# A two-layer decoder trunk with top-k experts: the experts' gate and spill loads asked for by ScalarE's queue, products and dots queued behind named work, one group fewer done ahead, index copies on VectorE

## The chip, the cores and the metric

The kernel runs on one core of one Trainium2 chip. The metric is the device time of one execution in microseconds (us). In the profile PE is TensorE, with its weight loads apart as PEld, DVE is VectorE, ACT is ScalarE, POOL is GpSimd and SP is SyncE, which in this kernel only asks for DMA transfers (rows of a queue itself are marked SPq, ACTq and so on).

## The reference

The input is one sequence of 512 tokens with 1024 channels. Two layers each have a mixer (pooling beside retention in layer 0, a gated linear recurrence in layer 1) and a PEER block; a layer norm closes each. The change lies in the PEER block:

```python
def block(xt):                                             # 128 tokens
    q = (xt @ w_q).reshape(T, PEER_HEADS, 2, PEER_HALF)    # 8 heads, 2 halves of 128
    s = jnp.einsum('thpd,hpkd->thpk', q, sub_keys)         # scores against 128 sub-keys
    s_top, i_top = lax.top_k(s, PEER_TOPK)                 # 16 best of each half
    cand = ...                                             # 16 x 16 sums, and their expert numbers
    best, pos = lax.top_k(cand, PEER_TOPK)                 # 16 best of 256
    eid = jnp.take_along_axis(cand_id, pos, axis=-1)       # one of 128*128 experts
    gate = jax.nn.softmax(best, axis=-1)
    act = gelu(jnp.einsum('td,thkd->thk', xt, u_tab[eid]))
    coef = gate * act
    return jnp.einsum('thk,thkd->td', coef, v_tab[eid])
```

Each token so takes part in 8 x 16 = 128 of the 16,384 experts. An expert is one row of `peer_u` (its dot with the token, then Gelu) and one row of `peer_v` (added to the output with the coefficient).

## The kernel before

Tokens stand in four blocks `tb` of 128. The experts of the first 384 tokens are computed densely: the 16,384 experts are 128 blocks of 128, four blocks make a group `g` (`NB` = 4, 32 groups). For every block, `mm1` multiplies 128 rows of `peer_u` with the tokens on TensorE (24 matmuls of 128x352, since each product is three products of high and low parts), and ScalarE's Gelu puts the activations into `ge`. `mm2` (L1084) later multiplies coefficients with 128 rows of `peer_v`: 18 matmuls of 128x512 a block, into six accumulators of PSUM that stay open over all 128 blocks. Rows of the two tables stream in through `stream`: SP asks for a block of 512 KB (`raw`, five buffers), ScalarE rounds it to `hi` (L168) and VectorE forms the rest `lo` (L169).

The last 128 tokens (`tb` = 3) are not dense: `gather_rounds` takes one expert of each token per round. GpSimd gathers 128 rows of `peer_u` (L967), VectorE takes the dots into a column of `av` (L978); after eight rounds ScalarE's Gelu and one multiply make the coefficients `cf` (L981, L982); GpSimd gathers the rows of `peer_v`, and VectorE accumulates them (L988) eight rounds after their dots. The first 32 tokens' activations come from a third path, `Scatter`: in the top-k stage, VectorE takes dots of gathered rows `urow` (L104), and GpSimd adds the gates into a table `gz` in memory.

A PEER block has these stages. `route_topk` (L766) goes through four chunks `c` of heads: projection of the queries (the copies `qh` of PSUM at L780 are ScalarE's), scores of four token blocks, top 16 by VectorE (L859 to L863), the copy of the indices to 16-bit floats `itop` (L864, ScalarE), and for `tb` = 1, 2, 3 some of the chunk's eight `Scatter` dots, which are to follow the last top-k instruction. `route_gates` (L882) then builds the dense gates of the other tokens with one-hot matmuls (L909, L910), scales them into `gbuf` (L911) and writes them to the table `gd` in memory (L915). Beside both, `lookahead` (L755) does `mm1` for the first `NLA` = 20 groups; it is advanced by one block for every 2.8 units of cost that the two stages hand out. Its `ge` are written to `sp` in memory (L763), but for the last two groups, which are kept.

`experts` (L991) then goes through all groups in an order that mixes the old ones with the 12 fresh ones, whose `mm1` is done here. `fetch` gets a group's data two groups ahead: `ge` from `sp` (L1022), gates from `gd` (L1024) and from `gz` (L137) into `gt`. For each pair of blocks VectorE multiplies `gt` by `ge` (L1050, the pair product), ScalarE rounds the result to `ch` (L168) and VectorE forms the rest `cl` (L169); with `hi` and `lo` these are what `mm2` reads. `gt` has three buffers, `ch` and `cl` two each. After each block, gather rounds are let in so that they end with the blocks.

The order of the instructions on each engine is set by a scheduler from the traced program. `with tc.issue_after(x)` forces each instruction that is traced inside, on the engine of `x`, to stand behind `x` in that engine's queue. An engine works through its queue in order, so an instruction that waits holds all behind it, DMA requests included.

Of the kernel before, what the change touches and what calls it, by code (L numbers as in the profile page):

```python
# [9 lines left out]
F32 = mybir.dt.float32  # L10
# [4 lines left out]
AF = mybir.ActivationFunctionType  # L15
ALU = mybir.AluOpType
# [4 lines left out]
P = 128  # L21
# [14 lines left out]
QN = P // NU  # L36
QC = 32 // QN
GQ = 8
NSD = TD // 32
NLA = 20  # L40
NSZ = 4
KEEP = 2
ROT = 3
# [98 lines left out]
class Kern:  # L142
# [623 lines left out]
    def route_topk(self, layer, xT, kT, gz):  # L766
        nc, tc, io = self.nc, self.tc, self.io
        with tc.tile_pool(name="rt", bufs=1) as rt, tc.tile_pool(name="rt2", bufs=2) as rt2, \
# [6 lines left out]
            itop = rt.tile([P, NTB, 16, 16], F16, name="itop", tag="itop")  # L775
# [65 lines left out]
            for c in range(4):  # L841
                qs = []
                keys = rt2.tile([P, 4, P], F32, name="keys", tag="keys")
                nc.sync.dma_start(out=keys, in_=io["keysT"][layer][:, c * 4:c * 4 + 4, :])
                self.proj_T(wq, c, xT, sink_q, early=c == 0)
                for tb in range(NTB):
                    ts = slice(tb * P, (tb + 1) * P)
                    ps = self.psB.tile([P, 512], F32, name="pB", tag="pB")
                    for i in range(4):
                        nc.tensor.matmul(ps[:, i * P:(i + 1) * P], qs[i][:, ts], keys[:, i, :],  # L850
                                         start=True, stop=True)
                    ixs = rs2.tile([P, 4, 16], U32, name="ix", tag="ix", bufs=2)
                    for i in range(4):
                        hp = c * 4 + i
                        sc = ps[:, i * P:(i + 1) * P]
                        mx = stop[:, tb, hp, :]
                        ix = ixs[:, i, :]
                        s2 = rs2.tile([P, P], F32, name="s2", tag="s2")
                        nc.vector.max(out=mx[:, 0:8], in_=sc)  # L859
                        nc.vector.max_index(out=ix[:, 0:8], in_max=mx[:, 0:8], in_values=sc)  # L860
                        nc.vector.match_replace(out=s2, in_to_replace=mx[:, 0:8], in_values=sc, imm_value=NEG)
                        nc.vector.max(out=mx[:, 8:16], in_=s2)
                        top = nc.vector.max_index(out=ix[:, 8:16], in_max=mx[:, 8:16], in_values=s2)  # L863
                    nc.scalar.copy(itop[:, tb, c * 4:c * 4 + 4, :], ixs)  # L864
                    yield YC[c]
                    if tb == 0:
                        yield from choose(0, c * 2, 2)
                        if c:
                            gz.add(self)
                    else:  # L870
                        n = (2, 3, 3)[tb - 1] * QC // 8
                        yield 1.3 * n
                        with tc.issue_after(top.ins):
                            gz.dots(self, n)
                gz.weigh(self, rs2)
                if c == 0:
                    gz.add(self)
# [80 lines left out]
    def gather_rounds(self, layer, main, ga):  # L958
        nc, io = self.nc, self.io
        eid, gate, x, acc = main  # L960
        jobs = list(range(P))
        coefs = []

        def row(name, job):
            t = ga.tile([P, D], F32, name="row", tag="row", bufs=6)
            at = eid[:, job:job + 1]
            nc.gpsimd.indirect_dma_start(out=t, out_offset=None, in_=io[name],  # L967
                                         in_offset=bass.IndirectOffsetOnAxis(ap=at, axis=0))
            return t

        for n in range(len(jobs) + GQ):
            if n < len(jobs):
                j = jobs[n]
                k = n % GQ
                if k == 0:
                    av = ga.tile([P, GQ], F32, name="av", tag="av", bufs=2)
                ur = row("u%d" % layer, jobs[n])
                nc.vector.tensor_tensor_reduce(ur, ur, x, 1.0, 0.0, ALU.mult, ALU.add, av[:, k:k + 1])  # L978
                if k == GQ - 1:
                    cf = ga.tile([P, GQ], F32, name="cf", tag="cf", bufs=2)  # L980
                    nc.scalar.activation(cf, av, AF.Gelu)  # L981
                    nc.vector.tensor_tensor(cf, cf, gate[:, j - k:j + 1], ALU.mult)  # L982
                    coefs.append(cf)
            if n >= GQ:
                i = n - GQ
                vr = row("v%d" % layer, jobs[i])
                c = coefs[i // GQ][:, i % GQ:i % GQ + 1]
                nc.vector.scalar_tensor_tensor(acc, vr, c, acc, ALU.mult, ALU.add)  # L988
            yield

    def experts(self, layer, xT, hs, gd, gz, sp, norm):  # L991
        nc, tc, io = self.nc, self.tc, self.io
        with tc.tile_pool(name="ex", bufs=2) as ex, tc.tile_pool(name="ga", bufs=2) as ga:
            ex.tile([P, 48], F32, name="gap", tag="gap")
            accs = [[(self.psC if hf else self.psB).tile([P, 512], F32, name="pC" if hf else "pB",
                                                          tag="pC" if hf else "pB") for hf in range(2)]
                    for _ in range(3)]
            rounds = self.gather_rounds(layer, (self.eid, self.gate3, self.x3, hs[3]), ga)
            total = NLA * NB * 1.0 + (NE - NLA * NB) * 2.0
# [13 lines left out]
            def fetch(n):  # L1013
                if n >= NG:
                    return
                g = order[n]
                if g in kept:
                    ge = self.kept[g]
                else:
                    ge = self.pe.tile([P, NB, TN], F32, name="ge", tag="ge", bufs=3)  # L1020
                if g < NLA and g not in kept:
                    nc.sync.dma_start(out=ge, in_=sp[g])  # L1022
                gt = ex.tile([P, NSD, NB, 32], F32, name="gt", tag="gt", bufs=3)
                nc.sync.dma_start(out=gt[:, NSZ:], in_=gd[g])  # L1024
                gz.read(nc.gpsimd if n < 2 else nc.sync, gt[:, :NSZ], g)
                ges[g] = (ge, gt)

            def front(i):
# [13 lines left out]
            for i in range(NE):  # L1042
# [4 lines left out]
                if i % 2 == 0:  # L1047
                    ge, gt = ges[g]
                    gf = gt[:, US:, b:b + 2, :]
                    nc.vector.tensor_tensor(gf, gf, ge[:, b:b + 2, :].rearrange("p b (s t) -> p s b t", t=32), ALU.mult)  # L1050
                    ch = ex.tile([P, 2, TD], F32R, name="ch", tag="ch")
                    cl = ex.tile([P, 2, TD], F32R, name="cl", tag="cl")
                    s4 = "p b (s t) -> p b s t"
                    cf = gt[:, :, b:b + 2, :].rearrange("p s b t -> p b s t")
                    mark = self.split(cf, ch.rearrange(s4, t=32), cl.rearrange(s4, t=32))
                    cs += [(ch[:, 0], cl[:, 0]), (ch[:, 1], cl[:, 1])]
                v = self.stream(io["peer_v"][layer, g * NB + b])
                vs.append(v)
# [2 lines left out]
                        for tb in range(3):  # L1061
                            self.mm2(accs[tb], tb, cs[k], vs[k], k == 0, False)
                used += 1.0 if g < NLA else 2.0
                while done < (P + GQ) * used / (total * 1.02):
                    done += 1
                    with tc.issue_after(mark.ins):
                        next(rounds, None)
            for _ in rounds:
                pass
            for tb in range(3):  # L1070
# [146 lines left out]
```

## Time and profile before

| | |
|---|---|
| Runs | 2842.74, 2844.35, 2854.67 us, median 2844.35 us |
| Profiled execution | 2857.61 us, its span 2855.8 us |
| Busy share of the span | PE 97%, PEld 86%, DVE 82%, POOL 47%, ACT 39% |
| Stages of layer 0 (us from the span's start) | mixer to 181, top-k 181 to 445, gates 445 to 622, change-over 622 to 649, experts 649 to 1367 |
| The same stages of layer 1 | to 1650, to 1920, to 2098, to 2126, to 2842 |

The ends of the stages are taken from the first and last matmuls of each stage; the change-over lies between the last gate matmul and the first `mm2`. TensorE is busy nearly throughout, so the idle time that counts is what stands ahead of its instructions. The other engines' busy shares say little by themselves: they matter where a matmul waits for them.

### The profile page before, as it was taken

To read this page: it belongs to the slowest core of one execution; us is meant where nothing else is said; L and a number is where in the kernel's file an instruction comes from. 1 tells how busy PE (TensorE), PEld (TensorE's weight loads), DVE (VectorE), ACT (ScalarE), POOL (GpSimd) and SP (SyncE) were. 2 spreads that over 40 slices of the span, in tenths; PEclk is the share of its full clock that TensorE was granted. 3 is DMA by queue.
4 is the path that set the end of the run, shared out by engine and by line. 5 is a ranking of instruction groups with operands and counts; after the bars stand their busy time and mean duration, and the time that the engine had idled before them with its cause. 6 is when DMAs were issued, how large, how long until landed. Compare 5 with 4: busy or idle time off the path is not lost.

```text
span 2855.8 us, 41883 instructions
## 1 busy us (share of the span) xinstructions
PE 2766.2 (97%) x15314; PEld 2451.5 (86%) x15314; DVE 2352.5 (82%) x4524; ACT 1111.9 (39%) x1607; POOL 1328.6 (47%) x865
## 2 busy tenths in 40 slices
PE   9999999999999999999999999998999999999998
PEld 7898899998888898788788888998998888787886
DVE  6777889868888787888797777898878887888888
ACT  3353346553333333333334343445543333333332
POOL 0005567764555544554000016667754554555552
PEclk9999999999999999999999999999999999999999
DMA  6457776999999998999222556676999999999995
GB/s 224 136 172 215 207 226 187 250 282 359 377 382 371 362 381 342 345 384 352 96 82 71 211 169 192 195 235 173 275 317 362 371 392 352 353 377 361 383 371 191
DMA packets 318895, 791.24 MB, mean 277 GB/s; under 512 B 62176, under 2 KB 128224, under 8 KB 318688
## 3 DMA queue, kind: packets, MB, share of 16 engines
q1 hardware_dynamic: 198560, 485.34, 47.4%
q0 software_dynamic: 120128, 303.22, 31.3%
q8 instruction: 120, 1.97, 0.3%
q14 instruction: 87, 0.71, 0.1%
HBM read 709.94 MB, written 78.51 MB: 276 GB/s over the span
## 4 chain that ended last, share of the span: by engine, by line
PE 47%; issue 22%; DVE 12%; DMA 12%; POOL 6%; ACT 1%; SPq 0%; DVEq 0%; POOLq 0%; ACTq 0%
PE pA L184 8%; PE pA L186 8%; PE pA L185 8%; POOL row L967 6%; DMA row<-in_v,eid 5%; PE pB L1084 5%; PE pC L1084 5%; DVE lo L169 3%; PE pC L184 3%; PE pC L185 3%; PE pC L186 3%; DMA gt<-gz 2%; DMA ge<-sp 2%; DVE row L978 1%; DVE h L988 1%
## 5 line engine op out<-in xcount | busy, mean ns | idle before, releaser
L168 ACT CAST hi<-raw 128x1024 fp32r<-128x1024 f32 (+1 forms) x609 | 634.4, 1049 | 767.1 <-DMA raw<-in_peer_v 303.5
L169 DVE TENSOR_TENSOR lo<-raw,hi 128x1024 fp32r<-128x1024 f32 (+1 forms) x609 | 731.4, 1216 | 135.2 <-ACT hi L168 111.5
L967 POOL DMA_INDIRECT row<-in_u,eid x256 | 390.4, 1525 | 548.9 <-DVE av L978 504.7
L186 PE MATMUL pA<-xThi,lo 128*128 128x352 f32 (+2 forms) x1840 | 620.2, 337 | 16.3 <-DVE lo L169 16.3
L184 PE MATMUL pA<-xThi,hi 128*128 128x352 f32 (+2 forms) x1840 | 624.4, 339 | 10.6 <-ACT qh L780 7.6
L185 PE MATMUL pA<-xTlo,hi 128*128 128x352 f32 (+2 forms) x1840 | 620.1, 337 | 0.7 <-DVE xTlo L169 0.7
L126 POOL DMA_INDIRECT gz<-gate,idx x256 | 484.6, 1893 | 137.9 <-issue 73.2
L967 POOL DMA_INDIRECT row<-in_v,eid x256 | 368.4, 1439 | 109.4 <-issue 59.1
L186 PEld LDWEIGHTS pA<-xThi,lo 128*128 128x128 f32 x1840 | 349.4, 190 | 35.1 <-DVE lo L169 20.2
L184 PEld LDWEIGHTS pA<-xThi,hi 128*128 128x128 f32 x1840 | 350.0, 190 | 30.5 <-ACT qh L780 8.5
L185 PEld LDWEIGHTS pA<-xTlo,hi 128*128 128x128 f32 x1840 | 349.8, 190 | 17.5 <-DVE xTlo L169 1.2
L988 DVE SCALAR_TENSOR_TENSOR h<-row,cf,h 128x1024 f32<-128x1024 f32 x256 | 329.1, 1286 | 35.9 <-DMA row<-in_v,eid 35.5
L1084 PE MATMUL pB<-hi,cl 128*128 128x512 f32 x768 | 303.9, 396 | 31.5 <-DVE cl L169 31.5
L978 DVE CUSTOM_DVE_ANT_0 row<-row,x 128x1024 f32<-128x1024 f32 x256 | 311.2, 1219 | 6.0 <-DMA row<-in_u,eid 5.8
L1084 PE MATMUL pB<-lo,ch 128*128 128x512 f32 x768 | 300.3, 391 | 3.9 <-DVE lo L169 3.9
L1084 PE MATMUL pB<-hi,ch 128*128 128x512 f32 x768 | 300.3, 391 | 1.4 <-ACT ch L168 1.4
L1084 PE MATMUL pC<-hi,cl 128*128 128x512 f32 x768 | 300.1, 391 | 0.0
L1084 PE MATMUL pC<-hi,ch 128*128 128x512 f32 x768 | 300.1, 391 | 0.0
L1084 PE MATMUL pC<-lo,ch 128*128 128x512 f32 x768 | 300.0, 391 | 0.0
L1050 DVE TENSOR_TENSOR gt<-gt,ge 128x704 f32<-128x704 f32 x128 | 111.4, 888 | 176.7 <-DMA gt<-gz 88.2
L168 ACT CAST ch<-gt 128x768 fp32r<-128x768 f32 x128 | 107.0, 836 | 272.4 <-DVE gt L1050 192.2
L740 POOL DMA_INDIRECT urow<-in_u,ids x64 | 74.9, 1170 | 292.0 <-ACT ids L86 196.5
(280 smaller groups left out, 4603.8 us busy)
## 6 DMA issues: line engine op xcount, KB each, us to landing
raw<-in_peer_ut SPq DMA_DIRECT2D x256, 512.0 KB, 6.4
raw<-in_peer_v SPq DMA_DIRECT2D x256, 512.0 KB, 7.6
gd<-gbuf SPq DMA_DIRECT2D x16, 2048.0 KB, 10.6
gt<-gd SPq DMA_DIRECT2D x64, 512.0 KB, 9.3
sp<-ge SPq DMA_DIRECT2D x36, 704.0 KB, 4.8
ge<-sp SPq DMA_DIRECT2D x36, 704.0 KB, 11.5
raw<-in_peer_w_q SPq DMA_DIRECT2D x32, 512.0 KB, 5.5
gz<-zero SPq DMA_DIRECT2D x64, 256.0 KB, 4.5
```

What stands on the lines that cost most here:

```text
L126: d = nc.gpsimd.indirect_dma_start(out=flat, out_offset=bass.IndirectOffsetOnAxis(ap=self.idx[c][:, j:j + 1], axis=0), in_=gate[:, j:j + 1 ...
L168: self.nc.scalar.copy(hi, src)
L169: return self.nc.vector.tensor_tensor(lo, src, hi.bitcast(F32), ALU.subtract)
L184: nc.tensor.matmul(ps, ah, bh, start=(first and i == 0), stop=False)
L185: nc.tensor.matmul(ps, ah, bl, start=False, stop=False)
L186: nc.tensor.matmul(ps, al, bh, start=False, stop=(last and i == n - 1))
L740: d = self.nc.gpsimd.indirect_dma_start(out=t, out_offset=None, in_=self.io["u%d" % layer], in_offset=bass.IndirectOffsetOnAxis(ap=ids[:, ...
L967: nc.gpsimd.indirect_dma_start(out=t, out_offset=None, in_=io[name], in_offset=bass.IndirectOffsetOnAxis(ap=at, axis=0))
L978: nc.vector.tensor_tensor_reduce(ur, ur, x, 1.0, 0.0, ALU.mult, ALU.add, av[:, k:k + 1])
L988: nc.vector.scalar_tensor_tensor(acc, vr, c, acc, ALU.mult, ALU.add)
L1050: nc.vector.tensor_tensor(gf, gf, ge[:, b:b + 2, :].rearrange("p b (s t) -> p s b t", t=32), ALU.mult)
L1084: nc.tensor.matmul(acc[hf], a[:, ts], b[:, hf * 512:(hf + 1) * 512], start=first and i == 0, stop=last and i == 2)
```

## The change

It has six parts.

1. `NLA` goes from 20 to 19: four blocks of `mm1` per layer move from `lookahead` into `experts`, and one group fewer is written to `sp` and read back.
2. The copy of the top-k indices to `itop` goes from ScalarE to VectorE (32 instructions).
3. The eight `Scatter` dots of a chunk are let in as 0, 4, 4 after the top-k of `tb` = 1, 2, 3, instead of 2, 3, 3.
4. In `gather_rounds`, Gelu and `cf` of eight dots are traced two rounds after the last dot, not at once, and the accumulation comes `LAG` = 12 rounds after its dot, not 8.
5. From the third group on, `fetch` asks for `ge`, `gd` and `gz` through ScalarE's queue, not SP's: 154 requests in the program.
6. The pair product stands in VectorE's queue behind the first gather dot after the previous pair's `cl`, or behind that `cl` where no dot follows.

```diff
-NLA = 20
+LAG = GQ + 4
+NLA = 19
...
-                    nc.scalar.copy(itop[:, tb, c * 4:c * 4 + 4, :], ixs)
+                    nc.vector.tensor_copy(itop[:, tb, c * 4:c * 4 + 4, :], ixs)
...
-                        n = (2, 3, 3)[tb - 1] * QC // 8
+                        n = (0, 1, 1)[tb - 1] * QC // 2
                         yield 1.3 * n
                         with tc.issue_after(top.ins):
                             gz.dots(self, n)
...
-        for n in range(len(jobs) + GQ):
+        for n in range(len(jobs) + LAG):
+            dot = None
...
-                nc.vector.tensor_tensor_reduce(ur, ur, x, 1.0, 0.0, ALU.mult, ALU.add, av[:, k:k + 1])
+                dot = nc.vector.tensor_tensor_reduce(ur, ur, x, 1.0, 0.0, ALU.mult, ALU.add, av[:, k:k + 1])
                 if k == GQ - 1:
-                    cf = ga.tile([P, GQ], F32, name="cf", tag="cf", bufs=2)
-                    nc.scalar.activation(cf, av, AF.Gelu)
-                    nc.vector.tensor_tensor(cf, cf, gate[:, j - k:j + 1], ALU.mult)
-                    coefs.append(cf)
-            if n >= GQ:
-                i = n - GQ
+                    dots.append((av, j - k))
+            if dots and n - dots[0][1] == GQ + 1:
+                a, j = dots.pop(0)
+                cf = ga.tile([P, GQ], F32, name="cf", tag="cf", bufs=2)
+                nc.scalar.activation(cf, a, AF.Gelu)
+                nc.vector.tensor_tensor(cf, cf, gate[:, j:j + GQ], ALU.mult)
+                coefs.append(cf)
+            if n >= LAG:
+                i = n - LAG
...
-            yield
+            yield dot
...
+                q = nc.scalar if n > 1 else nc.sync
                 if g < NLA and g not in kept:
-                    nc.sync.dma_start(out=ge, in_=sp[g])
+                    q.dma_start(out=ge, in_=sp[g])
                 gt = ex.tile([P, NSD, NB, 32], F32, name="gt", tag="gt", bufs=3)
-                nc.sync.dma_start(out=gt[:, NSZ:], in_=gd[g])
-                gz.read(nc.gpsimd if n < 2 else nc.sync, gt[:, :NSZ], g)
+                q.dma_start(out=gt[:, NSZ:], in_=gd[g])
+                gz.read(q if n > 1 else nc.gpsimd, gt[:, :NSZ], g)
...
-                    nc.vector.tensor_tensor(gf, gf, ge[:, b:b + 2, :].rearrange("p b (s t) -> p s b t", t=32), ALU.mult)
+                    with ExitStack() as after:
+                        if i:
+                            after.enter_context(tc.issue_after(turn.ins))
+                        nc.vector.tensor_tensor(gf, gf, ge[:, b:b + 2, :].rearrange("p b (s t) -> p s b t", t=32),
+                                                ALU.mult)
...
-                    mark = self.split(cf, ch.rearrange(s4, t=32), cl.rearrange(s4, t=32))
+                    turn = mark = self.split(cf, ch.rearrange(s4, t=32), cl.rearrange(s4, t=32))
...
-                while done < (P + GQ) * used / (total * 1.02):
+                while done < (P + LAG) * used / (total * 1.02):
                     done += 1
                     with tc.issue_after(mark.ins):
-                        next(rounds, None)
+                        dot = next(rounds, None)
+                    if turn is mark and dot is not None:
+                        turn = dot
```

Lines after the first edits stand a little lower in the changed kernel: L1050 becomes L1059, L1084 becomes L1096, L1022 and L1024 become L1028 and L1030, L168 and L169 become L169 and L170.

Three places show how the queues change. The first is VectorE early in the experts stage of layer 0. Before, three products stand close together, one on `gt_7157` and two on the next group's `gt_7544` (the numbers tell the buffers of different groups apart), and only behind them the `cl` that reads `gt_7157`:

```order
L169 TENSOR_TENSOR lo_7485<-raw_7482,hi_7484 128x1024
L988 SCALAR_TENSOR_TENSOR h3_87<-row_7539,cf_7216,h3_87 128x1024
L169 TENSOR_TENSOR lo_7497<-raw_7494,hi_7496 128x1024
L1050 TENSOR_TENSOR gt_7157<-gt_7157,ge_7156 128x11x64
L1050 TENSOR_TENSOR gt_7544<-gt_7544,ge_7542 128x11x64 x2
L169 TENSOR_TENSOR lo_7555<-raw_7552,hi_7554 128x1024
L169 TENSOR_TENSOR cl_7549<-gt_7157,ch_7548 128x768
```

Now a product is followed by its own `cl`, and a gather dot (L980) stands between a `cl` and the next product:

```order
L170 TENSOR_TENSOR lo_7719<-raw_7716,hi_7718 128x1024
L1059 TENSOR_TENSOR gt_7402<-gt_7402,ge_7400 128x11x64
L170 TENSOR_TENSOR lo_7756<-raw_7753,hi_7755 128x1024
L170 TENSOR_TENSOR lo_7768<-raw_7765,hi_7767 128x1024
L170 TENSOR_TENSOR cl_7750<-gt_7402,ch_7749 128x768
L980 ISA row_7759,av_7487<-row_7759,x3_1031 128x1024
L980 ISA av_7487 128x1
L993 SCALAR_TENSOR_TENSOR h3_87<-row_7762,cf_7539,h3_87 128x1024
L170 TENSOR_TENSOR lo_7810<-raw_7807,hi_7809 128x1024
L1059 TENSOR_TENSOR gt_7402<-gt_7402,ge_7400 128x11x64
L170 TENSOR_TENSOR cl_7873<-gt_7402,ch_7872 128x768
```

No product of a later group stands ahead of the `cl` any more, and the two products on `gt_7402` have the first one's `cl` and a dot between them.

The second place is the queue that asks for the gates, in the same stage. Before, SP's queue has them between the table's blocks:

```order
L174 DMA raw_8521<-in_peer_ut 128x1024
L1024 DMA gt_8363<-gd0_1024 128x1024
L137 DMA gt_8363<-gz0_1420 128x512
L174 DMA raw_8558<-in_peer_v 128x1024
L174 DMA raw_8570<-in_peer_v 128x1024
```

Now they stand in ScalarE's queue between the roundings:

```order
L169 CAST ch_7477<-gt_7027 128x768
L169 CAST hi_7574<-raw_7572 128x1024
L1030 DMA gt_7552<-gd0_1024 128x1024
L138 DMA gt_7552<-gz0_1420 128x512
L169 CAST hi_7621<-raw_7619 128x1024
L169 CAST hi_7633<-raw_7631 128x1024
L169 CAST ch_7556<-gt_7151 128x768
```

The request for `gt_7552` now follows the `ch` of the group whose buffer it takes (`gt_7027`), with one rounding between them.

The third place is TensorE where layer 0 goes over from the gates to `mm2`. Before, a whole block of `mm1` begins behind the last gate matmul (L910):

```order
L909 MATMUL pC<-og,oh 128x128
L910 LDWEIGHTS oh
L910 MATMUL pC<-og,oh 128x128
L184 MATMUL pC<-xThi,hi 128x352
L185 MATMUL pC<-xTlo,hi 128x352
```

Seven blocks follow there, 168 matmuls, and then the first `mm2`. Now:

```order
L910 MATMUL pC<-og,oh 128x128
L911 LDWEIGHTS oh
L911 MATMUL pC<-og,oh 128x128
L187 MATMUL pA<-xThi,lo 128x352
L185 MATMUL pA<-xThi,hi 128x352
L186 MATMUL pA<-xTlo,hi 128x352
```

Here the last matmul of a block and three blocks follow, 73 matmuls, ahead of the first `mm2`: the blocks taken from `lookahead` are missing at this place, and the gates stage ahead of it has 1847 matmuls of `mm1` where it had 1848 (counted from the start of top-k).

More of the change, by code (lines that the diff above doesn't have):

```diff
@@ L961, in gather_rounds @@
         jobs = list(range(P))
-        coefs = []
+        coefs, dots = [], []
         def row(name, job):
```

## The prediction, made before the changed kernel was run

> **What bounds the kernel now.** I read the page's first lines, then the stages one by one, then who waits for whom on TensorE, and only then the engines that keep it waiting.
>
> ```profile
> span 2855.8 us, 41883 instructions
> PE 2766.2 (97%) x15314; PEld 2451.5 (86%) x15314; DVE 2352.5 (82%) x4524; ACT 1111.9 (39%) x1607; POOL 1328.6 (47%) x865
> 181.00:445.00 264.00, 254.70 (x1499) 239.37 (x1498) 215.93 (x907) 108.95 (x182) 143.66 (x91) 0.98 0.69 201
> 622.00:649.00 27.00, 26.77 (x171) 26.48 (x169) 10.21 (x12) 9.14 (x15) 8.03 (x8) 1.00 0.97 333
> 649.00:1367.00 718.00, 700.11 (x3366) 601.01 (x3367) 612.02 (x711) 245.34 (x302) 372.33 (x250) 1.00 0.93 360
> 1650.00:1920.00 270.00, 260.74 (x1540) 244.89 (x1539) 217.79 (x918) 112.01 (x186) 144.57 (x92) 0.98 0.68 199
> 2126.00:2842.00 716.00, 696.72 (x3358) 598.88 (x3357) 609.37 (x710) 241.04 (x296) 373.95 (x250) 1.00 0.92 356
> 1214.73 0.39 PE L1084 MATMUL pB<-lo,ch 128*128 128x512 f32 x1
> 1214.96 0.39 PE L1084 MATMUL pC<-lo,ch 128*128 128x512 f32 x1
> 612.01 0.32 PE L186 MATMUL pC<-xThi,lo 128*128 128x352 f32 x1
> 612.17 0.32 PE L184 MATMUL pC<-xThi,hi 128*128 128x352 f32 x1
> PE pB L1084 <- DVE cl L169: 31.5, 29, 2.3
> PE pA L186 <- DVE lo L169: 16.3, 7, 4.2
> PE pA L184 <- ACT qh L780: 7.6, 2, 3.8
> ```
>
> In a row of a window stand its ends, its length, the busy time (and instructions) of PE, PEld, DVE, ACT and POOL, the granted clock, the DMA engines' busy share and GB/s. A row of a wait has its sum, how often it came, and the longest.
>
> TensorE bounds it, at 97%. Its floor in the experts stage: 128x512 matmuls start 0.23 us apart, 128x352 ones 0.16 us (over longer stretches of such rows 0.227 and 0.159). The stage has 128 x 18 = 2304 of the first and 44 x 24 = 1056 of the second (four of the 48 fresh blocks come before it): 523.0 + 167.9 = 690.9 us. It took 718 and 716, so 27 and 25 us were lost, 52 in all. What ends most of the waits there is `cl`, and this leads to VectorE's queue:
>
> ```profile
> L1050 DVE TENSOR_TENSOR gt<-gt,ge 128x704 f32<-128x704 f32 x64 | 55.7, 888 | 90.4 <-DMA gt<-gz 46.2 <-DMA ge<-sp 34.1 <-issue 10.1
> 681.92 0.89 DVE L1050 TENSOR_TENSOR gt<-gt,ge 128x704 f32<-128x704 f32 x1 [6.64 <-DMA gt<-gz]
> 682.73 0.95 DVE L169 TENSOR_TENSOR cl<-gt,ch 128x768 fp32r<-128x768 f32 x1
> ```
>
> The first row groups one layer's experts stage: ahead of 64 products VectorE stood idle for 90 us, most of it for transfers into `gt` and `ge`. The other two show the damage: a product waits 6.64 us for gates, and the `cl` that stands directly behind it in the queue has to wait with it, then TensorE. VectorE is busy for 612 of 718 us, so it has 106 us of slack, and it spends 90 of them in these places.
>
> **The change part by part.**
>
> *Top-k (parts 2 and 3).* The losses sit in a few places:
>
> ```profile
> 220.00:232.00 12.00, 7.79 (x22) 5.59 (x21) 10.04 (x33) 1.55 (x3) 3.56 (x3) 0.72 0.79 258
> 290.00:311.00 21.00, 15.92 (x61) 12.06 (x60) 16.46 (x54) 4.88 (x12) 14.58 (x9) 0.92 0.72 208
> 1690.00:1704.00 14.00, 9.95 (x41) 7.52 (x39) 9.66 (x33) 2.00 (x5) 4.49 (x4) 0.88 0.79 258
> 1764.00:1782.00 18.00, 13.46 (x45) 9.94 (x44) 14.54 (x47) 4.88 (x12) 13.79 (x8) 0.81 0.71 210
> 226.03 0.80 PE L186 MATMUL pA<-xThi,lo 128*128 128x512 f32 x1 [4.21 <-DVE lo L169]
> DVE urow L104 <- DMA urow<-in_u,ids: 41.1, 13, 8.3
> 302.99 0.24 ACT L864 CAST itop<-ix 128x64 f16<-128x64 uint32 x1 [7.53 <-DVE ix L863]
> 303.14 0.58 ACT L780 COPY qh<-pA 128x512 f32<-128x512 f32 x1
> L864 ACT CAST itop<-ix 128x64 f16<-128x64 uint32 x32 | 7.8, 244 | 111.2 <-DVE ix L863 111.2
> ```
>
> In these four windows PE is idle for 4.2, 5.1, 4.1 and 4.5 us, and it goes on at less clock: (1 - 0.72) x 12 = 3.4 us, then 1.7, 1.7 and 3.4; 28 us together. There are two causes. VectorE waits for a gathered `urow` ahead of its dot, with `lo` behind it (the 4.21). And ScalarE waits 7.53 us for indices in order to copy them, with `qh` behind. Part 3 lets the first dots in one token block later, which is 264 / 16 = 16.5 us, against a longest wait for a row of 8.3: most rows will have landed. Part 2 takes the copy off ScalarE. On VectorE it stands behind the instruction that makes the indices and waits for nothing; 32 copies of 0.24 are 8 us in two stages where VectorE has (264 - 216) + (270 - 218) = 100 us of slack, so I cost them at nothing; without that cover they would be 8. Ends: 28 us back, or 5, if only `qh` comes free and the dots wait elsewhere. I take 20, nearer the upper end, since both causes stand in rows by name.
>
> *One group fewer ahead (part 1).* 4 x 24 x 0.159 = 15.3 us of `mm1` per layer only move. But they move out of the change-over, where they covered something:
>
> ```profile
> 622.56 0.62 ACT L911 ACTIVATE gbuf<-pC 128x512 f32<-128x512 f32 x1
> 623.21 0.38 SPq L915 DMA_DIRECT2D gd<-gbuf  x1
> 632.75 1.27 SPq L1024 DMA_DIRECT2D gt<-gd  x3
> 641.70 1.69 DVE L1050 TENSOR_TENSOR gt<-gt,ge 128x704 f32<-128x704 f32 x2 [5.95 <-DMA gt<-gz]
> 647.19 0.89 DVE L1050 TENSOR_TENSOR gt<-gt,ge 128x704 f32<-128x704 f32 x1
> 648.11 0.83 ACT L168 CAST ch<-gt 128x768 fp32r<-128x768 f32 x1 [5.65 <-DVE gt L1050]
> 649.00 0.50 PE L1084 MATMUL pB<-hi,ch 128*128 128x512 f32 x1 [0.23 <-ACT ch L168]
> sp<-ge SPq DMA_DIRECT2D x36, 704.0 KB, 4.8
> ```
>
> The last gates are scaled (622.56), written (623.21), landed and read back (632.75), landed again (641.70), multiplied and rounded (by 649.0). From the last gate matmul, at 622.0, until 649.0 TensorE had 168 matmuls, 26.7 us, and so no gap. Now it has 73, 11.6 us. The path gets shorter too, since the product that is needed first no longer stands behind others: 641.7 + 0.89 + 0.83 is 643.4, or 21.4 us after the last gate matmul. So TensorE will stand for 21.4 - 11.6 = 9.8 us in each layer, and then lose some clock: 1.7 us by the second window above, 3.4 by the first. With 1.7 it is 11.5, or 23 for both layers. The two ends: with 3.4, +26; and if the way back lands in 4.8 us (the spills' median, the last row) and not in the 641.7 - 632.75 = 9.0 seen here, +14. I take +22, next to what the rows of this place give.
>
> [...]
>
> *Gate requests, product order, later Gelu (parts 4, 5, 6).* The product moves behind the previous pair's `cl` and a dot, so it can't hold back earlier `cl`. The gates are asked for two groups ahead, and a group takes 718 / 32 = 22 us; the transfers need
>
> ```profile
> ge<-sp SPq DMA_DIRECT2D x36, 704.0 KB, 11.5
> gt<-gd SPq DMA_DIRECT2D x64, 512.0 KB, 9.3
> gt<-gz SPq DMA_DIRECT2D x60, 256.0 KB, 10.4
> SPq L1024 <- DVE cl L169: 36.4, 55, 1.3
> ACT cf L981 <- DVE av L978: 222.8, 29, 11.8
> ```
>
> from request to landing (the last number, a median): 9 to 12 us, half of one group. So most of the products' waits should go. On ScalarE the requests wait for the last `cl` of the buffer's old group, as they waited on SP (0.66 us each by the fourth row), and the roundings `hi` and `ch` stand behind: 60 groups make 40 us. The issue of 154 requests has no row on ScalarE; on SP three took 1.27 us, so 65 us. Against both, ScalarE is idle for (718 - 245) + (716 - 241) = 948 us of the two stages, and gets back much of the 222.8 us in which it stood at a Gelu for the last dots; part 4 costs nothing else, as the rounds still end with the blocks. So I cost these waits at nothing; if the lead of the five `raw` buffers doesn't cover them, the 40 us count (a rival below). What is late next is VectorE with its 612 us and four more `lo`, then the DMA engines with 0.93 of 718, 668 us; both stay below TensorE's 691 + 15. Ends: all 52 us back, or 10, half of the 52 - 31.5 that isn't named `cl`. I take 36: the 31.5, and a little of the clock lost behind it.
>
> *Sum.* -20 + 22 - 36 = -34 on the profiled execution's 2857.6, so 2824. The median of the runs is 13.3 us below that execution. A single profile can't say where those lie; if they are waits of the same kind, the median run has less to win. I take 4 off: -30 on 2844.35, **2814 us**. The terms' mean distances from their ends (12, 6, 21), combined as independent ones, make 25; since both far ends need other causes than the ones named, I use 22: 2792 to 2836. What a measurement of this kernel can tell from no change is about 0.5%, 14 us.
>
> **Rivals.** *The gates land no sooner* (R1).
>
> ```profile
> 1214.00:1244.00 30.00, 30.00 (x148) 26.14 (x148) 27.28 (x32) 10.05 (x11) 19.42 (x14) 1.00 1.02 416
> ```
>
> In such stretches the DMA engines have no time left, and then the issuer hardly matters: the product waits as before, a place later, and its own `cl` is late. Experts 0, top-k -20, change-over +22: 2846. Against it: in just this stretch TensorE is busy throughout (30.00 of 30).
>
> [...]
>
> *ScalarE is held at the requests* (R2, the slower side). A request stands one or two roundings behind the last `ch` of the buffer's old group, and waits for a `cl` that VectorE reaches in its own order. If `hi` or `ch` is late for `mm2` by 1 us each time (SP's longest wait of this kind was 1.3), 60 groups cost 60: -20 + 22 - 36 + 60 = +26, 2870. It decides from 34 / 60 = 0.57 us a group on. Against it stands ScalarE's idle time, for it that roundings can't pass a request.
>
> *The change-over stays covered* (R3). If both landings take 4.8 us and not 9.5 and 9.0, the path is 12.5 us and the gap 0.9: +2 in place of +22, with the rest as forecast 2794. Against it: 0.97 of the DMA engines' time was taken there; for it, that the moved blocks' loads leave the place.
>
> **How the numbers follow.** Forecast 0.60, R1 0.17, R2 0.12, R3 0.11. Five sixths of the forecast lie below 2830 (0.50), the rest within 0.5%. Faster: 0.50 + 0.11 = 0.61; within 0.5%: 0.10 + 0.17 = 0.27; slower: 0.12. The range holds the forecast and R1 and leaves out R2 and the best of R3: 2786 to 2850.
>
> **What would show it.** Experts: idle time ahead of the products under 25 us a layer (90.4 now), TensorE's waits for `cl` under 12 us (31.5), each stage near 718 + 15 - 18 = 715 us with the four blocks in it. Top-k: no matmul waits for `qh`, and the clock stays at 1.0 at the four windows' places. Change-over: TensorE idle for 8 to 11 us ahead of the first `mm2`, then a clock below 1. It would be wrong if that gap were small, if roundings stood behind requests with `mm2` waiting for them, or if the products' waits only moved behind the dots.

## The result, and the profile after

The changed kernel takes 2803.56 us (median of four runs, 2803.44 to 2805.55) against 2844.11 us (median of the kernel before with one run more than in its table): 40.5 us less. The ratio on record is 0.9851, 95% interval 0.9827 to 0.9875; the two medians by themselves make 0.9857. The forecast was 2814 us, 30 less. Of all the runs in this document one is left out, a run of the last kernel below that took 3387.51 us at a granted clock of 0.752.

The page's first lines and the start of its chain for the changed kernel:

```profile
span 2801.9 us, 41670 instructions
PE 2745.8 (98%) x15314; PEld 2449.4 (87%) x15314; DVE 2359.3 (84%) x4556; ACT 1116.5 (40%) x1575; POOL 1352.6 (48%) x865
PE 86%; DVE 7%; DMA 3%; POOL 2%; issue 1%; ACT 1%; SPq 0%; DVEq 0%; POOLq 0%; ACTq 0%
```

The chain of work that ended last is TensorE's for 86% of the span, where it was 47%. From the starts of the last gate matmul, the first `mm2` and the last `mm2` of each layer, the time divides as follows (us; the experts stage of the changed kernel contains 15.3 us of `mm1` that lay ahead of it before):

| | before | changed | difference |
|---|---|---|---|
| Layer 0, to the last gate matmul | 621.9 | 612.6 | -9.3 |
| Layer 0, change-over | 27.1 | 19.3 | -7.8 |
| Layer 0, experts | 718.3 | 708.9 | -9.4 |
| Layer 1, from there to the last gate matmul | 730.5 | 719.0 | -11.5 |
| Layer 1, change-over | 27.8 | 21.6 | -6.2 |
| Layer 1, experts | 716.7 | 707.3 | -9.4 |

Together -53.6 us between the two profiled executions. The one of before lies 13 us above the median of its runs, the one of the changed kernel at its median, hence the 40.5 between the medians.

At the four places of the top-k stages where the prediction found its losses, the changed kernel has these rows:

```profile
217.00:229.00 12.00, 10.23 (x50) 8.23 (x49) 11.01 (x32) 2.32 (x4) 7.98 (x4) 1.00 0.90 302
280.00:301.00 21.00, 17.70 (x80) 14.28 (x79) 18.73 (x52) 3.30 (x8) 16.58 (x10) 1.00 0.83 278
1663.00:1682.00 19.00, 17.52 (x82) 14.37 (x81) 18.24 (x52) 4.00 (x6) 8.81 (x5) 1.00 0.92 312
1722.00:1740.00 18.00, 14.72 (x67) 12.78 (x67) 12.36 (x39) 3.41 (x6) 10.27 (x8) 0.83 0.89 301
```

TensorE's idle time and lost clock there, 28 us before, are 12.9 us now: 9.8 idle, and (1 - 0.83) x 18 = 3.1 of clock, all of it in the last window. In that window VectorE still stands 6.5 us for a gathered row, and a matmul 3.3 us for `lo`.

The rows of the groups for products and `cl` in the experts stage of layer 0:

```profile
L170 DVE TENSOR_TENSOR cl<-gt,ch 128x768 fp32r<-128x768 f32 x64 | 61.0, 953 | 57.7 <-ACT ch L169 57.7
L1059 DVE TENSOR_TENSOR gt<-gt,ge 128x704 f32<-128x704 f32 x64 | 56.7, 885 | 3.4 <-DMA gt<-gz 3.4
```

VectorE's idle time ahead of the products fell from 90.4 to 3.4 us. It is still idle, now for 57.7 us ahead of `cl`, until ScalarE has made `ch`: but that is the end of a chain in the right order, and no matmul waits for this `cl`. The waits of TensorE's instructions, largest first, and the windows of the change-overs and experts:

```profile
PE pA L187 <- DVE lo L170: 11.2, 7, 3.3
PE pB L1096 <- DMA raw<-in_peer_ut: 9.7, 1, 9.7
PE pB L1096 <- ACT ch L169: 8.2, 2, 7.4
PE pC L834 <- DVE ka L954: 3.4, 1, 3.4
612.70:632.00 19.30, 11.88 (x77) 11.59 (x74) 5.94 (x6) 6.27 (x10) 6.79 (x7) 0.90 0.92 313
632.00:645.00 13.00, 12.25 (x46) 9.48 (x47) 10.05 (x15) 2.25 (x3) 6.99 (x6) 0.89 1.03 413
2081.00:2094.00 13.00, 12.71 (x47) 10.36 (x48) 10.71 (x15) 3.10 (x4) 6.52 (x6) 0.83 1.02 410
631.90:1341.00 709.10, 708.35 (x3465) 616.79 (x3465) 620.08 (x718) 253.51 (x306) 381.23 (x251) 1.00 0.95 368
2081.30:2788.60 707.30, 707.30 (x3455) 616.46 (x3456) 617.68 (x716) 248.97 (x300) 376.62 (x251) 1.00 0.94 364
```

No wait for `cl` is left among them (31.5 us before). Two new ones stand at the change-overs, 7.4 and 9.7 us, each with a lower granted clock behind it: (1 - 0.89) x 13 = 1.4 us and (1 - 0.83) x 13 = 2.2 us. The path that ends the first of them, from the timeline:

```profile
613.58 0.38 SPq L916 DMA_DIRECT2D gd<-gbuf  x1
622.93 0.80 SPq L1030 DMA_DIRECT2D gt<-gd  x2
630.07 0.89 DVE L1059 TENSOR_TENSOR gt<-gt,ge 128x704 f32<-128x704 f32 x1 [3.44 <-DMA gt<-gz]
630.99 0.83 ACT L169 CAST ch<-gt 128x768 fp32r<-128x768 f32 x1 [5.25 <-DVE gt L1059]
631.88 0.80 PE L1096 MATMUL pB<-hi,ch 128*128 128x512 f32 x1 [7.42 <-ACT ch L169]
```

The write takes 9.3 us to land, the way back 7.1, product and rounding 1.8. In layer 1 the wait is put down to a table block, `raw<-in_peer_ut`; but `ch` ended at 2081.24 there and the matmul began at 2081.29, so it is the same path.

### The profile page after: what moved, and what is told of

Same layout as the page of the kernel before. It is cut to its first block, busy times and chain, and to the rows that moved or that the text cites. A ratio compares the mean times of both kernels' runs of the same rounds, so it can differ in the third digit from the quotient of the medians.

```text
span 2801.9 us, 41670 instructions
## 1 busy us (share of the span) xinstructions
PE 2745.8 (98%) x15314; PEld 2449.4 (87%) x15314; DVE 2359.3 (84%) x4556; ACT 1116.5 (40%) x1575; POOL 1352.6 (48%) x865
## 4 chain that ended last, share of the span: by engine, by line
PE 86%; DVE 7%; DMA 3%; POOL 2%; issue 1%; ACT 1%; SPq 0%; DVEq 0%; POOLq 0%; ACTq 0%
PE pB L1096 18%; PE pC L1096 18%; PE pA L187 12%; PE pA L185 12%; PE pA L186 12%; PE pC L185 2%; PE pC L186 2%; PE pC L187 2%; POOL gz L127 2%; DMA urow<-in_u,ids 2%; DVE lo L170 1%; PE pB L910 1%; DMA gd<-gbuf 1%; PE pB L911 1%; PE pB L851 1%
## 5 line engine op out<-in xcount | busy, mean ns | idle before, releaser
L169 ACT CAST hi<-raw 128x1024 fp32r<-128x1024 f32 (+1 forms) x609 | 637.8, 1050 | 962.9 <-PE pC L1096 368.2
L170 DVE TENSOR_TENSOR lo<-raw,hi 128x1024 fp32r<-128x1024 f32 (+1 forms) x609 | 733.7, 1215 | 184.5 <-ACT hi L169 156.4
L187 PE MATMUL pA<-xThi,lo 128*128 128x352 f32 (+2 forms) x1872 | 628.7, 336 | 11.2 <-DVE lo L170 11.2
L185 PE MATMUL pA<-xThi,hi 128*128 128x352 f32 (+2 forms) x1872 | 631.2, 337 | 0.6 <-ACT hi L169 0.3
L968 POOL DMA_INDIRECT row<-in_u,eid x256 | 407.3, 1591 | 464.4 <-DVE av L980 369.2
L186 PE MATMUL pA<-xTlo,hi 128*128 128x352 f32 (+2 forms) x1872 | 627.4, 335 | 0.6 <-DVE xTlo L170 0.6
L968 POOL DMA_INDIRECT row<-in_v,eid x256 | 361.9, 1414 | 145.1 <-issue 58.5
L980 DVE CUSTOM_DVE_ANT_0 row<-row,x 128x1024 f32<-128x1024 f32 x256 | 311.6, 1219 | 10.0 <-DMA row<-in_u,eid 9.7
L1096 PE MATMUL pB<-hi,ch 128*128 128x512 f32 x768 | 300.2, 391 | 17.9 <-DMA raw<-in_peer_ut 9.7
L1096 PE MATMUL pC<-hi,ch 128*128 128x512 f32 x768 | 299.9, 390 | 0.0
L1096 PE MATMUL pC<-lo,ch 128*128 128x512 f32 x768 | 299.6, 390 | 0.0
L1096 PE MATMUL pB<-hi,cl 128*128 128x512 f32 x768 | 299.6, 390 | 0.0
L1096 PE MATMUL pB<-lo,ch 128*128 128x512 f32 x768 | 299.5, 390 | 0.0
L1096 PE MATMUL pC<-hi,cl 128*128 128x512 f32 x768 | 299.3, 390 | 0.0
L170 DVE TENSOR_TENSOR cl<-gt,ch 128x768 fp32r<-128x768 f32 x128 | 122.0, 953 | 117.0 <-ACT ch L169 117.0
L741 POOL DMA_INDIRECT urow<-in_u,ids x64 | 86.9, 1358 | 273.4 <-ACT ids L87 203.7
L169 ACT CAST ch<-gt 128x768 fp32r<-128x768 f32 x128 | 107.2, 837 | 249.4 <-PE pC L1096 152.2
```

The lines of the kernel that those rows point to most:

```text
L169: self.nc.scalar.copy(hi, src)
L170: return self.nc.vector.tensor_tensor(lo, src, hi.bitcast(F32), ALU.subtract)
L185: nc.tensor.matmul(ps, ah, bh, start=(first and i == 0), stop=False)
L186: nc.tensor.matmul(ps, ah, bl, start=False, stop=False)
L187: nc.tensor.matmul(ps, al, bh, start=False, stop=(last and i == n - 1))
L741: d = self.nc.gpsimd.indirect_dma_start(out=t, out_offset=None, in_=self.io["u%d" % layer], in_offset=bass.IndirectOffsetOnAxis(ap=ids[:, ...
```

## The experiments

Each kernel was timed beside the kernel before on the same chip. The kernel before varies over 16 us among its runs (2842.5 to 2858.6), those with the products' order over 8 at most; so the undone parts are read against the changed kernel's 2803.6. The changed kernel itself was not timed again beside them, and they ran on three chips, so a difference of some 4 us from 2803.6 is not told from none.

**Part 1 undone.**

```diff
-NLA = 19
+NLA = 20
```

> The changed kernel with 20 groups ahead as before (part 1 undone, all else kept). In the trace of the changed kernel TensorE stands 7.4 us (layer 0) and 9.7 us (layer 1) ahead of the first mm2. Theory: with 168 matmuls of mm1 in the change-over again (26.7 us) against a path of 19 to 22 us both gaps close and nothing else changes: 2803.6 - 17 = about 2787 us. Rival: the group done later also relieves the experts stage, through 1.4 MB less spill traffic a layer and one old group less; then the experts lose about what the change-over wins: 2800 to 2806 us.

Measured: 2781.14 us, 0.9757 of before (0.9733 to 0.978), 22.4 us under the changed kernel. The windows from the last gate matmul to the first `mm2` and over the experts stage, for both layers:

```profile
611.70:638.40 26.70, 26.70 (x173) 26.70 (x171) 9.40 (x10) 10.65 (x16) 9.16 (x9) 1.00 0.97 328
638.40:1330.30 691.90, 691.47 (x3369) 600.34 (x3368) 615.40 (x713) 248.10 (x300) 372.98 (x250) 1.00 0.96 374
2048.50:2075.20 26.70, 26.70 (x173) 26.70 (x171) 10.03 (x11) 10.62 (x16) 12.39 (x12) 1.00 0.98 326
2075.20:2765.20 690.00, 690.00 (x3361) 599.66 (x3360) 612.49 (x711) 244.36 (x294) 378.49 (x249) 1.00 0.95 370
```

TensorE is busy for all of 26.7 us in both change-overs. The theory holds, with 5 us more than its 17: in the profiles the change-overs give 7.7 and 10.0 us (19.3 - 11.6 and 21.6 - 11.6), the experts stages 1.7 and 2.0 behind the gaps (693.6 against 691.9 and 692.0 against 690.0, the moved 15.3 taken off), and the stages up to the gates 0.9 and 0.8. Less spill traffic brought nothing.

**Part 5 undone.**

```diff
-                q = nc.scalar if n > 1 else nc.sync
+                q = nc.sync
```

> The changed kernel with all requests for gates and spills asked for by SP again (part 5 undone; GpSimd keeps gz of the first two groups). Theory: the order of the products (part 6) carries the gain in the experts stage, and who asks matters little: 2801 to 2809 us, idle time ahead of the products under 15 us a layer. Rival: the request on ScalarE is what brings the gates in time; on SP they stand behind table blocks that wait for buffers, the products wait 30 to 90 us a layer again, and with them cl: 2825 to 2845 us.

Measured: 2800.71 us, 0.9824 of before (0.9801 to 0.9848). The interval overlaps the changed kernel's, and the time is 0.3 us below the theory's range. Behind the change-over of layer 0 the products wait for nothing:

```profile
L1059 DVE TENSOR_TENSOR gt<-gt,ge 128x704 f32<-128x704 f32 x63 | 55.7, 884 | 0.0
```

Once the products stand in order, it doesn't matter who asks.

**Part 6 undone.**

```diff
-                        if i:
+                        if False:
                             after.enter_context(tc.issue_after(turn.ins))
```

> The changed kernel with the pair product free to stand anywhere (part 6 undone). Theory: products stand ahead of earlier cl again and wait there for the gates; most of the 49 us that the experts stages won are lost: 2834 to 2850 us, with 20 us or more of waits of mm2 for cl. Rival: what counts is that ScalarE asks earlier; the gates have landed wherever the product stands: 2800 to 2810 us.

Measured: 2830.56 us, 0.9929 (0.9905 to 0.9953), 27 us above the changed kernel.

```profile
L1059 DVE TENSOR_TENSOR gt<-gt,ge 128x704 f32<-128x704 f32 x63 | 54.4, 885 | 57.9 <-DMA gt<-gz 46.9 <-DMA ge<-sp 11.0
PE pB L1096 <- DVE cl L170: 19.4, 6, 5.9
ACT hi L169 <- DVE cl L170: 56.2, 9, 11.2
ACT ge L754 <- DVE cl L170: 47.1, 6, 11.2
```

The waits are back, 57.9 us in layer 0 and not 90.4, and the stages take 725.1 and 720.2 us: 29 of the 49 us are lost. The rival, that earlier requests free the products wherever they stand, falls. Without the order ScalarE also stands for `cl`, with the requests in its queue, for 103 us in all (the last two rows); in the changed kernel it has no such wait. The time is 3.4 us better than the theory's range: some 20 us of the 49 stayed, which led to the next runs.

**Parts 2 and 3 undone.**

```diff
-                    nc.vector.tensor_copy(itop[:, tb, c * 4:c * 4 + 4, :], ixs)
+                    nc.scalar.copy(itop[:, tb, c * 4:c * 4 + 4, :], ixs)
...
-                        n = (0, 1, 1)[tb - 1] * QC // 2
+                        n = (2, 3, 3)[tb - 1] * QC // 8
```

> The changed kernel with the index copy on ScalarE and the dots at 2, 3, 3 (parts 2 and 3 undone). Theory: the top-k and gate stages lose the 9.3 and 11.5 us that they won: 2803.6 + 21 = about 2824 us, with matmuls that wait for qh for 3 to 4 us again. Rival: those stalls depend on where the rest of the program puts the blocks of mm1, and come out otherwise now: 2801 to 2812 us.

Measured: 2823.79 us, 0.9899 (0.9875 to 0.9923), 20 us above the changed kernel, as the theory has it. The gates end at 624.2 us, and 728.4 us behind layer 0's end (612.6 and 719.0 in the changed kernel), and the matmuls that wait for `qh` are back:

```profile
PE pA L185 <- ACT qh L781: 7.6, 2, 3.8
```

**Part 4 undone.**

```diff
-LAG = GQ + 4
+LAG = GQ
...
-            if dots and n - dots[0][1] == GQ + 1:
+            if dots and n - dots[0][1] == GQ - 1:
```

> The changed kernel with Gelu and cf traced right after the last of eight dots and the accumulation 8 rounds after its dot, as before (part 4 undone). Without the products' order (part 6 undone, run above) the experts stages still won 20 of 49 us, and the requests' queue (part 5 undone) was worth nothing, so: theory, those 20 us are part 4's own, because ScalarE no longer stands at a Gelu with roundings behind it; undone, 2815 to 2825 us, and ScalarE's waits for av go back above 150 us. Rival: once the products stand right, VectorE reaches the dots in time and a Gelu's wait is covered by ScalarE's slack: 2802 to 2809 us.

Measured: 2803.99 us, 0.9843 (0.982 to 0.9865): the rival. ScalarE's wait at the Gelu stays gone without part 4:

```profile
ACT cf L986 <- DVE av L980: 22.3, 16, 2.5
```

It was 222.8 us before. The dots were late because VectorE was held at products, so the products' order mends this too: with part 6 alone in the kernel before (below) it is 22.3 us as well.

**Parts 1 and 5 undone** (the two edits above together).

> The changed kernel with 20 groups ahead and the requests on SP (parts 1 and 5 undone, parts 2, 3, 4, 6 kept). Theory: the two are independent: 2781 for the first, 3 us less for the second as the run with part 5 undone had it: 2776 to 2782 us. Rival: with the change-over covered the experts run at their floor only because ScalarE asks; on SP, 34 us of waits come back: above 2790 us.

Measured: 2780.72 us, 0.9769 (0.9749 to 0.9788), as the theory has it. Beside 2781.14 it shows once more that the queue is worth nothing.

**Part 6 alone,** in the kernel before: the `issue_after` around the product, `turn`, and the dot that a round hands back, as in the diff of the change.

> The kernel before with the products' order alone (part 6 alone; 20 groups, requests on SP, Gelu at once, top-k as before). Theory (part 4 has 20 us of its own): the experts stages win about 29 us, the time is 25 to 33 us under that of the kernel before on the same chip. Rival (the order carries nearly all): 42 to 52 us under it.

Measured: 2801.31 us against 2847.3 in the same runs, 0.9843 (0.9823 to 0.9863), 46 us less: the rival. The experts windows:

```profile
649.00:1339.90 690.90, 690.90 (x3369) 600.42 (x3368) 614.18 (x711) 248.81 (x300) 374.88 (x250) 1.00 0.96 374
2092.20:2782.20 690.00, 690.00 (x3361) 599.67 (x3360) 611.64 (x711) 244.25 (x294) 375.39 (x250) 1.00 0.95 371
L1054 DVE TENSOR_TENSOR gt<-gt,ge 128x704 f32<-128x704 f32 x64 | 56.9, 889 | 0.0
```

In the profiled execution, the fastest of the four (2797.48 us), TensorE never stops, and the products wait 0.0 us in layer 0. One edit recovers all that the stage had lost.

**Part 5 alone,** in the kernel before.

```diff
+                q = nc.scalar if n > 1 else nc.sync
...
-                nc.sync.dma_start(out=gt[:, NSZ:], in_=gd[g])
-                gz.read(nc.gpsimd if n < 2 else nc.sync, gt[:, :NSZ], g)
+                q.dma_start(out=gt[:, NSZ:], in_=gd[g])
+                gz.read(q if n > 1 else nc.gpsimd, gt[:, :NSZ], g)
```

(`ge` likewise.)

> The kernel before with the requests on ScalarE alone (part 5 alone). Theory: nothing, within 8 us of the kernel before on the same chip, with 150 us or more of idle time ahead of the products in both layers. Rival: asking earlier removes a good part of the products' waits by itself: 15 us or more under the kernel before. The slower side: ScalarE is held both by Gelu and by the requests, 10 us or more above it.

Measured: 2876.59 us against 2847.3, 1.0108 (1.0075 to 1.014), 29 us slower. It is the slower side: ScalarE is held. Waits of ScalarE and TensorE, and a piece of the timeline:

```profile
ACT hi L168 <- DVE cl L169: 83.6, 15, 10.3
ACT ge L753 <- DVE cl L169: 54.5, 6, 10.7
PE pB L1085 <- DVE lo L169: 19.9, 4, 5.7
1132.39 0.33 ACTq L1025 DMA_DIRECT2D gt<-gd  x1
1133.25 0.47 ACT L753 ACTIVATE ge<-pA 128x352 f32<-128x352 f32 x1 [10.71 <-DVE cl L169]
1133.29 1.37 ACTq L1023 DMA_DIRECT2D ge<-sp  x1
1148.24 2.50 DVE L1051 TENSOR_TENSOR gt<-gt,ge 128x704 f32<-128x704 f32 x3 [11.26 <-DMA ge<-sp]
1150.82 0.83 ACT L168 CAST ch<-gt 128x768 fp32r<-128x768 f32 x1 [12.99 <-DVE gt L1051]
1151.92 0.79 PE L1085 MATMUL pB<-lo,ch 128*128 128x512 f32 x1 [5.74 <-DVE lo L169]
```

ScalarE stood 10.71 us for `cl` ahead of the request at 1132.39; so the request for `ge` behind it came only at 1133.29; so the product waited 11.26 us for `ge`, until 1148.24; ScalarE stood 12.99 us for that product; and at the end `lo`, which stood behind that product on VectorE, was late for TensorE by 5.74 us. Two queues wait for each other in turn.

**Part 2 undone.** Only the index copy is back on ScalarE; the dots stay at 0, 4, 4.

> The changed kernel with the index copy on ScalarE again (part 2 undone; the dots stay at 0, 4, 4). Parts 2 and 3 together were worth 20 us. Theory: the two matmuls that wait 3.8 us each for qh come back, with 1.7 to 3.4 us of slow clock behind each: 2803.6 + 11 to 14 = 2814 to 2818 us, the rest of the 20 being part 3's. Rival: with the first dots later VectorE makes the indices earlier, the copy no longer waits long, and qh stays in time: 2801 to 2808 us.

Measured: 2799.7 us, 0.9804 (0.9776 to 0.9833): the rival, 1 us below its range. ScalarE still waits at the copies, but no matmul for `qh`:

```profile
ACT itop L865 <- DVE ix L864: 62.9, 24, 11.2
PE pA L187 <- DVE lo L170: 9.2, 6, 2.4
280.00:301.00 21.00, 19.90 (x95) 16.60 (x94) 17.57 (x49) 4.52 (x11) 15.19 (x9) 1.00 0.91 295
```

With the dots moved, the copies' waits fall from 111.2 to 62.9 us, and the window around 290 us keeps its clock. What held the indices in the kernel before stands 21 us ahead of the copy that waited 7.53 us, at the first dot of the token block before:

```profile
281.44 1.22 DVE L104 CUSTOM_DVE_ANT_0 urow<-urow,xx 128x1024 f32<-128x1024 f32 x1 [8.32 <-DMA urow<-in_u,ids]
```

VectorE stood 8.32 us there for a gathered row, and from 283.7 us on worked without a gap until it had the indices at 302.9. In the run without part 2 VectorE's longest stand for a gathered row is 3.9 us; a copy still waits up to 11.2 us, but `qh` is in time for TensorE. Part 2 adds nothing to part 3; part 2 alone was not tried.

**Part 4 alone,** in the kernel before.

> The kernel before with Gelu two rounds after the last dot and the accumulation 12 rounds after its dot (part 4 alone). With the requests on ScalarE and the products unordered, the experts stages lose 36 us each against their floor without part 4 and 19 and 14 with it (two runs above). Theory: Gelu holds ScalarE also when SP asks, and the roundings behind it are late: 10 to 25 us under the kernel before on the same chip. Rival: it matters only where ScalarE has to ask for the gates: within 6 us of it, with 150 us of idle time ahead of the products as before.

Measured: 2863.33 us against 2852.7, 1.004 (1.0026 to 1.0055): slightly slower, and neither the theory nor the rival. ScalarE's wait at Gelu hardly moves, and the products wait as before:

```profile
ACT cf L986 <- DVE av L980: 210.8, 32, 13.0
L1059 DVE TENSOR_TENSOR gt<-gt,ge 128x704 f32<-128x704 f32 x64 | 55.2, 885 | 83.3 <-DMA gt<-gz 51.9 <-DMA ge<-sp 31.4
```

Two rounds more don't help while VectorE is held. Why parts 4 and 5 together (the run with part 6 undone) won some 20 us in the experts stages, where each alone won nothing, stays open; that run had parts 1 to 3 as well. ScalarE's wait at Gelu was 89.2 us in it, against 167.3 us with part 5 alone, so the two may act together, but no run has parts 4 and 5 without the others.

**Parts 2, 3 and 6 alone,** in the kernel before.

> The kernel before with the index copy on VectorE, the dots at 0, 4, 4, and the products' order (parts 2, 3 and 6; 20 groups, requests on SP, Gelu at once). Theory: parts 4 and 5 add nothing, since the experts stages stand at their floor with the order alone, and part 1 costs: 2777 to 2785 us. Rival: part 4 or 5 is needed once the top-k moves the blocks of mm1: above 2790 us.

Measured: 2781.98 us, 0.9743 (0.9716 to 0.977). The theory holds. This, like the two other runs with 20 groups, the order and the top-k parts (part 1 undone; parts 1 and 5 undone), is about 22 us faster than the changed kernel, and the three can't be told from one another.

**As that, with all eight dots after the third token block.**

```diff
-                        n = (0, 1, 1)[tb - 1] * QC // 2
+                        n = (0, 0, 1)[tb - 1] * QC
```

> As the run with parts 2, 3 and 6 alone, but the eight dots of a chunk all after the third token block's top-k (0, 0, 8). In the run with 20 groups and requests on SP, VectorE still stood 6.54 us for urow ahead of the first of four dots, and a matmul behind lo 2.6 us later. Theory: by then all rows have landed; 5 to 10 us under that run. Rival: eight dots in a row (10 us) hold lo themselves: the same or up to 10 us above it.

Measured: 2786.83 us, 0.9768 (0.9733 to 0.9803), 5 us above the run before it (2786.4 to 2789.7 us against 2779.6 to 2783.3): the rival.

```profile
PE pC L187 <- DVE lo L170: 11.1, 2, 5.6
PE pB L851 <- ACT qh L781: 7.3, 2, 3.8
```

Two matmuls wait 11.1 us together for a `lo` that stands behind the eight dots, and two 7.3 us for `qh`. The theory's premise doesn't hold either, since not all rows had landed: VectorE still stood 28 times for the row of a dot, 35.1 us in all and 2.5 us at most.

## Why the prediction was right, point by point

- *What bounds it.* The floor of 690.9 us came out within 1 us: the order alone runs layer 0's stage in 690.9 us, layer 1's in 690.0. TensorE stayed the bound; VectorE's 618 to 620 us and the DMA engines' 0.95 fit below it.
- *Top-k, -20.* Measured -9.3 and -11.5 in the profile, 20 us by the run with both parts undone. The size was right, one of the two causes wasn't: the `qh` waits were put down to the index copy on ScalarE, but they go with the dots. The copy waited 7.53 us because VectorE, held at a gathered row 21 us earlier, made the indices late. What a wait's row names is the last link; the cause lay one link further. That the size came out is partly luck: the four places gave 15 of their 28 us, and by the last score matmuls (414.1 and 405.0 us in layer 0; 520.6 and 513.9 behind layer 0's end in layer 1) 15.8 of the 20.8 us were won; the other 5 came behind them, nearly all in layer 1, where the term counted nothing. And one sign failed: at the fourth place the clock is 0.83, not 1.0, because a row still came 6.5 us late for its dot. One token block of time was not enough for all rows.
- *Change-over, +22.* Gaps of 7.4 and 9.7 us against 9.8 forecast, the path 19.3 and 21.6 against 21.4, and the whole of part 1 cost 22.4. The slow clock behind the gaps came to 1.4 and 2.2 us by the windows above; the forecast's 1.7, read from before's second top-k window (a clock of 0.92 over 21 us), lies between them.
- *Experts, -36.* This term was mis-sized: it measured -49.4 by the table, and -53.0 as the prediction counts it, with the 3.6 us of clock behind the gaps in the change-over's term (which is then +20.2). That lies beyond the upper end of 52. The signs named for it came: VectorE stands 3.4 and 5.8 us ahead of the products (25 was the limit), and no matmul waits for `cl`. I kept about three quarters of the 20 us that the waits for `cl` didn't hold, as a loss of other kind. The order alone takes them away too, so they went with the same stalls: of the 53 us between before's two stages (718 and 716) and those of the order alone (690.9 and 690.0), 37 were idle time of TensorE (17.9 and 19.3), and the other 16 longer matmuls (busy 700.1 and 696.7 against 690.9 and 690.0). How much of these 16 was clock is not shown; the rows give 1.00 for both stages.
- *Who carries it.* Parts 4, 5 and 6 stood as one term. Part 6 is enough for all of it (-46 alone); parts 4 and 5 are worth nothing beside it (+0.4 and -2.9 us when undone). It is not the only way to a part of it: with part 6 undone the rest still held some 20 us, for a reason that stays open.
- *The requests at nothing, with their cover named.* The cover was real, but it was the products' order, and not ScalarE's idle time or the five `raw` buffers, which were there with and without it: in the changed kernel ScalarE has no wait for `cl` (the prediction counted 40 us of it), with the order undone 103 us. In the kernel before, with part 5 alone, a hold of R2's kind cost 29 us and not 60, half a microsecond a group; but what `mm2` waited for was VectorE's `lo` and `cl` (19.9 and 25.2 us), not ScalarE's `hi` or `ch`.
- *R1* did not happen: the products' waits went with the order, and no later `cl` was late. That the issuer hardly matters, which it started from, came out in the runs that have the products' order: 2803.56 and 2800.71 us, 2781.14 and 2780.72 us with the one issuer and the other.
- *R3* didn't happen: the landings took 9.3 and 7.1 us in layer 0 and 11.2 and 7.6 in layer 1 (requests at 2060.68 and 2071.87 us, product at 2079.49), not 4.8.
- *The 4 us taken off* for the difference between the profiled execution and the median went the right way but was too small: the profiles differ by 53.6 us, the medians by 40.5, so all of the 13 should have come off. That they were stalls of the kind that the change removes fits this, but before's median run has no profile to show it. The forecast's closeness is in part luck: on the profiles the terms were 19.6 us too small (0.8, 1.8 and 17.0), and the 9 us too little taken off hid half of that.

## What to carry to other kernels

An instruction that waits for a transfer should stand in its engine's queue no earlier than the work that is needed before it; here one such ordering edge, put in alone, was worth 46 us, and moving the transfer's request was worth nothing with it and cost 29 us without. Before work is moved out of a stage, see what it covers there: four blocks that seemed only to move had covered a 20-us path through memory, and putting them back gave 22 us. And where a matmul waits for a copy, follow the copy's own wait one step back before moving it to another engine.

## What the runs showed of the hardware that was not expected

The times of the kernel with these stalls scatter more: the kernel before took 2842.5 to 2858.6 us over all its runs, and the four beside the changed kernel lie 12 us apart, while the changed kernel's four lie within 2.1 us. It is a tendency only, since with the order in and the Gelu at once (part 4 undone) four runs lie 7.7 us apart. A ratio with the kernel before so depends on the draw, and one profiled execution of it lay 13 us off its median.
